# Stick-breaking attention by summation by parts, in a streaming encoder layer on one core

## The chip, the cores and the metric

The kernel runs on one core of a Trainium2 chip. Times are device microseconds from the core's run; lower is better. The engines are TensorE (PE; PEld is its weight load), VectorE (DVE), ScalarE (ACT), GpSimd (POOL) and SyncE (SP), which issues every DMA of this kernel.

## The reference

One layer of an encoder over 1,024 prompt frames and 64 frames of a running stream, 1,088 tokens in all, everything in float32. A mixer (three branches: stick-breaking attention, spatial gating, memory cross-attention) is followed by a feed-forward sublayer. The attention has 8 heads of 128 channels:

```python
def stick_breaking(q, k, v, q_pos, k_pos):
    # A[t,s] = beta_ts * prod_{s<j<t}(1-beta_tj), s < t only
    z = einsum('bqhd,bkhd->bhqk', q, k) * (SB_HEAD_DIM ** -0.5)
    mask = k_pos[None, :] < q_pos[:, None]
    log_keep = where(mask, log_sigmoid(-z), 0.0)
    between = cumsum(log_keep, axis=3, reverse=True) - log_keep
    w = where(mask, exp(log_sigmoid(z) + between), 0.0)
    return einsum('bhqk,bkhd->bqhd', w, v)
```

A prompt query sees the prompt keys before it. A sample query sees 256 cached keys and values and the sample's own before it. The new key and value rows are outputs too.

## The kernel before

Every instruction is emitted into a fixed order per engine by a program that runs while the kernel is built: it keeps a clock for each engine and one for the DMA bus (`Clocks`, with costs of its own), and places background work (`stream`, `breathe`, `later`) where those clocks say its inputs are ready. An engine then runs its instructions in that order and stops at the first whose inputs have not come. All instructions are recorded at line 75, the wrapper that accounts for them, so the rows are told apart by tile names.

**Projection.** The input projection is done in units of 256 output columns (`strassen_unit`): the seven products of a Strassen step, each of many matmuls into one of three PSUM buffers (`pb`), which DVE (and for the first product ACT) adds up into two row tiles `c[0]`, `c[1]` of 128 channels by 1,088 tokens. Weights arrive as two raw loads of 512 KB per unit, some products ahead, and ACT and DVE split them into a high and a low part (`whl`). The order of the projections is: gating values, gating input, memory queries, attention keys, attention values (four units, a pair of heads each), attention queries, gates.

**Values.** After a unit of attention values, `v_out` transposes each head's row tile to tokens on partitions (`transposed`: nine 128x128 blocks on PE, copied by ACT to a tile `tm` called `o` in the code). Then `fin` stores the output rows, stores the sample's 64 rows to `v8S`, and splits the 128x1,024 prompt part into a high and a low part (`vrh`, `vrl`), which go to DRAM (`vS`) and come back when the head is attended to.

**Attention.** `sb_all` runs 48 items, 8 heads by 6 batches of query blocks (128 queries each, as many keys as lie before them; the ninth block has 320 keys for the sample). In order of emission each step of the loop has: `z` of item n (scores on PE into PSUM, then ACT writes `pr` = sigmoid of the negated scores, which is the keep factor, and `beta` = sigmoid of the scores, and POOL zeroes the masked part of the diagonal blocks of `beta`), `trp` of item n-3 (PE transposes the weights; ACT copies the high part `ath`, DVE subtracts the low part `atl`), `scan` of item n-1 (DVE: a reverse running product of `pr`, which a mask resets to 1 at and beyond each query's position, then `beta` times the scanned product of the next key), and `av` of item n-4 (PE: weights times values; ACT writes `osb`). `sb_load` fetches the next head's keys, queries and values at its predecessor's first item, `sb_prep` prepares the cached keys at the third.

The last items run in the background of the branch projections that follow. Those are dense on TensorE, as is the feed-forward part.

Tiles come from rings of slots (`A`: 40 large slots, `U`: 11 small ones); a slot is used again when its last reader is done.

Of the kernel before, what the change touches and what calls it, by code (L numbers as in the profile page):

```python
# [9 lines left out]
F32 = mybir.dt.float32  # L10
F32R = mybir.dt.float32r
AF = mybir.ActivationFunctionType
ALU = mybir.AluOpType
AX = mybir.AxisListType

P = 128
T = 1088
# [67 lines left out]
class Clocks:  # L85
# [43 lines left out]
    def at(self, *tiles):  # L129
        return max([self.wrote.get(x.tensor.name, (0,))[0] for x in tiles], default=0) + self.LATENCY  # L130
# [16 lines left out]
def encoder_layer(  # L147
# [14 lines left out]
    clock, at = clocks.t, clocks.at  # L162
    nc = Engines(tc.nc, clocks)
    ctx.enter_context(tc.manual_schedule())

    keep = ctx.enter_context(tc.tile_pool(name="keep", bufs=1))
# [7 lines left out]
    def nm(s):  # L174
        cnt[0] += 1
        return f"{s}_{cnt[0]}"

    def A(shape, dt=F32, s="a"):
        return arena.tile(shape, dt, tag="s", name=nm(s), bufs=NSLOT)

    def U(shape, dt=F32, s="u"):
        return arena.tile(shape, dt, tag="u", name=nm(s), bufs=NSMALL)
# [17 lines left out]
    def dtile(shape, s):  # L200
        return dram.tile(shape, F32, tag=s, name=s)

    def f32(ap):
        return ap.bitcast(F32)
# [4 lines left out]
    def load(dst, src):  # L209
        nc.sync.dma_start(dst, src)  # L210

    def store(dst, src):
        nc.sync.dma_start(dst, src)

    def act(out, in_, f=AF.Copy, **kw):
        nc.scalar.activation(out, in_, f, **kw)

    def sub(out, a, b):
        nc.vector.tensor_tensor(out, a, b, op=ALU.subtract)
# [4 lines left out]
    def mul(out, a, b):  # L224
        nc.vector.tensor_tensor(out, a, b, op=ALU.mult)
# [19 lines left out]
    def tp(out, in_):  # L245
        n = in_.shape[0]
        nc.tensor.transpose(out, in_, ident[:n, :n])
# [7 lines left out]
    c_gmem, c_gpre, c_gffn, c_lng, c_lnb = [cols[:, 8 * i:8 * i + 8] for i in range(5)]  # L255
    c_gate = cols[:, 40:64]
    c_gpm, c_gpf = cols[:, 64:72], cols[:, 72:80]
    ones1 = keep.tile([P, 1], F32, tag="ones1", name="ones1")
    nc.vector.memset(ones1, 1.0)

# [6 lines left out]
    vS = [[dtile([P, 1024], f"vS{r}{p}") for p in "hl"] for r in range(8)]  # L267
    v8S = [dtile([64, P], f"v8S{r}") for r in range(8)]
# [14 lines left out]
    def later(n, fn, src=()):  # L283
        due.append((max([clock[e] for e in ("pe", "act", "dve")]) + 2.5 * n if n else at(*src), fn))
# [10 lines left out]
    def stream(*stages):  # L295
        st = list(stages)
        streams.append(st)
        return st
# [567 lines left out]
    def tm_store(dst_p, dst_s, h, o):  # L866
        store(dst_p[0, 0, :, h, :].rearrange("(j p) d -> p j d", p=P), o[:, :8, :])
        store(dst_s[0, 0, :, h, :], o[64:, 8, :])
# [12 lines left out]
    def v_out(p):  # L881
        def consume(c):
            for m in range(2):
                h = 2 * p + m

                def fin(o, h=h):
                    tm_store(sb_v_prompt, sb_v_sample, h, o)
                    store(v8S[h], o[64:, 8, :])
                    hi, lo = A([P, 1024], F32R, "vrh"), A([P, 1024], F32, "vrl")
                    ov = o[:, :8, :].rearrange("p j d -> p (j d)")  # L890
                    act(hi, ov)
                    sub(lo, ov, f32(hi))

                    later(0, lambda: store(vS[h][0], f32(hi)), [hi])
                    later(0, lambda: store(vS[h][1], lo), [lo])
                transposed(c[m], fin)
        return consume

# [827 lines left out]
    def sb_load(h):  # L1726
        s = SB[h] = {}
        for n, src, w in (("k", kT, T), ("q", qT, T), ("vv", vS, 1024)):
            pair = []
            for i in range(2):  # L1730
                t = A([P, w], F32, n)
                load(t, src[h][i])
                pair.append(f32r(t))
            s[n] = pair
            if n == "k":
                c = s["c"] = U([P, 4, P], F32, "sbc")
                load(c[:, :2], cache_sb_k[0, 0, :, h, :].rearrange("(m p) d -> p m d", p=P))
        load(c[:, 2:], cache_sb_v[0, 0, :, h, :].rearrange("(m p) d -> p m d", p=P))
        s["vv"] = [t.rearrange("p (j d) -> p j d", j=8) for t in s["vv"]]
        x = A([P, 768], F32, "ksv")  # L1740
        s["ks"] = f32r(x[:, :640]).rearrange("p (s m) -> p s m", s=2)
        s["v8"] = x[:, 640:]
        nc.gpsimd.memset(x[:64, 640:], 0.0)
        load(x[64:, 640:], v8S[h])

    def sb_prep(h):
        s = SB[h]
        t = PT()
        for m in range(2):
            tp(t[:, m * P:(m + 1) * P], s["c"][:, m, :])  # L1750
        ks = s["ks"]
        split(t[:, :256], ks[:, 0, :256], ks[:, 1, :256])
        for i in range(2):
            nc.gpsimd.tensor_copy(ks[:, i, 256:], f32(s["k"][i][:, 1024:]))
        s["prep"] = True


    BATCH = [[(0, 0), (2, 128), (1, 512)], [(3, 0), (8, 512)], [(4, 0)], [(5, 0)], [(6, 0)], [(7, 0)]]

    def length(i):  # L1760
        return 320 if i == 8 else (i + 1) * P
# [17 lines left out]
    def sb_all():  # L1779
        scale = 128 ** -0.5  # L1780
        masks = sb_masks()
        Ps, As, ATs, osb = {}, {}, {}, {}

        def z(h, b):
            s = SB[h]
            qh, ql = s["q"]
            pt = PB()
            base = 0
            L = sum(length(i) for i, _ in BATCH[b])
            for i, c in BATCH[b]:  # L1790
                kh, kl = s["k"] if i < 8 else (s["ks"][:, 0, :], s["ks"][:, 1, :])
                Li = length(i)
                qa = i * P if i < 8 else T - P

                parts = 1 if Li <= 512 else 2
                w = Li // parts
                wm = max(w, 256)
                if parts == 2:
                    base = 512 - w
                for q in range(parts):  # L1800
                    o = base + c + q * w
                    mm3(pt[:, o:o + wm], qh[:, qa:qa + P], ql[:, qa:qa + P], kh[:, q * w:q * w + wm],
                        kl[:, q * w:q * w + wm], True, True)
            beta = A([P, 1024], F32, "beta")
            pr = A([P, 1024], F32, "pr")
            zz = pt[:, base:base + L]
            act(pr[:, :L], zz, AF.Sigmoid, scale=-scale)
            act(beta[:, :L], zz, AF.Sigmoid, scale=scale)
            for i, c in BATCH[b]:
                dg = beta[:, c + length(i) - P:c + length(i)]  # L1810
                nc.gpsimd.affine_select(out=dg, in_=dg, pattern=[[-1, P]], base=0, channel_multiplier=1,
                                        compare_op=ALU.is_gt, fill=0.0)
            Ps[h, b], As[h, b] = pr, beta

        def scan(h, b):

            pr, beta = Ps.pop((h, b)), As[h, b]
            L = sum(length(i) for i, _ in BATCH[b])
            nc.vector.tensor_tensor_scan(pr[:, :L][:, ::-1], pr[:, :L][:, ::-1], masks[b][:, ::-1], 1.0,
                                         op0=ALU.mult, op1=ALU.max)  # L1820
            mul(beta[:, :L - 1], beta[:, :L - 1], pr[:, 1:L])

        def trp(h, b):
            a = As.pop((h, b))
# [35 lines left out]
        def av(h, g):  # L1860
            s = SB[h]
            pt = PT()
            if h not in osb:
                osb[h] = A([P, T], F32, "osb")
            if g == 8:
                f = ATs.pop((h, 8))
                for j in range(3):
                    vv = s["c"][:, 2 + j, :] if j < 2 else s["v8"]
                    nc.tensor.matmul(pt[:, :P], lhsT=vv, rhs=f[:, j, :], start=j == 0, stop=j == 2)
                act(osb[h][:, 1024:], pt[:, 64:P])  # L1870
                return
            vh, vl = s["vv"]
            at = ATs.pop((h, g))
            nb = 2 * g + 2
            for j in range(nb):
                hi, lo = at[j // 4]
                mm3(pt[:, :256], vh[:, j, :], vl[:, j, :], hi[:, j % 4, :], lo[:, j % 4, :], j == 0, j == nb - 1)
            act(osb[h][:, g * 256:(g + 1) * 256], pt[:, :256])
            if g == 3:
                o = osb.pop(h)  # L1880
                del SB[h]

                def put():
                    store(osc[0][h], o)
                    if h == 7:
                        O_READY[0] = 0
                later(0, put, [o])
# [6 lines left out]
        for n in range(N + SB_LAG + 1):  # L1894
            at_item[0] = n
            if n < N:
                h, b = items[n]
# [18 lines left out]
            if 0 <= n - SB_LAG - 1 < N:  # L1916
                h, b = items[n - SB_LAG - 1]
# [21 lines left out]
    for j in range(2):  # L1939
        d = {}  # L1940
# [12 lines left out]
    pt = PT()  # L1953
# [7 lines left out]
    for n, i in enumerate([0, 1, 2, 3, 8, 4, 5, 6, 7]):  # L1961
        def ld(i=i):
            H[i] = load_tile(i, x_prompt[0], x_sample[0])
        d = {}
# [105 lines left out]
```

## Time and profile before

| | us |
|---|---|
| median of 3 runs | 2312.54 |
| the runs | 2310.91 to 2314.28 |
| the profiled execution's own time | 2308.9 |
| its span, first to last instruction | 2306.3 |
| TensorE busy in the span | 2218.2 (96%) |
| VectorE busy in the span | 1600.3 (69%) |

The profile is of one execution. Shares of the whole span are averages over stages with different limits: the attention stage lies at about 960 to 1190 us, the projection of its values at about 450 to 560 us.

### The profile page before, as it was taken

How to read it: one execution, taken by the hardware profiler on the slowest of the kernel's cores; microseconds unless marked ns; L12 is line 12 of the kernel's file. 1: busy time of each engine (PE TensorE's matmuls, PEld its weight loads, DVE VectorE, ACT ScalarE, POOL GpSimd, SP SyncE). 2: the span in 40 equal slices, each digit the busy share in tenths (PEclk: the TensorE clock that was granted, in tenths of full speed). 3: DMA queues.
4: the chain of work that ended last, by engine and by line, in shares of the span. 5: the costliest groups of instructions: out<-in, count | busy, mean ns of one | idle time of the engine just before them, and what ended most of it. 6: DMA issues, size and time to landing. Idle time of an engine off the chain costs nothing. (4 is left out here: it accounts for less than half of the span.)

```text
span 2306.3 us, 40728 instructions
## 1 busy us (share of the span) xinstructions
PE 2218.2 (96%) x16465; PEld 2144.9 (93%) x16465; DVE 1600.3 (69%) x2483; ACT 781.4 (34%) x1383; POOL 143.8 (6%) x236
## 2 busy tenths in 40 slices
PE   7899999999999999988899999996999999999998
PEld 6799999999999999887799999996999999998886
DVE  7955688867776666699953443569777777774677
ACT  8442222333212223677731121344211111134353
POOL 2000000000000000134200000122000000000000
PEclk9999999999999999999999999998999999999999
DMA  6523356765393328654444352332323332247335
GB/s 206 183 89 101 123 207 208 230 202 199 144 298 133 113 86 287 254 205 165 143 159 128 112 170 86 104 108 92 94 83 104 94 102 87 92 159 275 83 106 187
DMA packets 249535, 345.97 MB, mean 150 GB/s; under 512 B 17140, under 2 KB 184644, under 8 KB 249348
## 3 DMA queue, kind: packets, MB, share of 16 engines
q1 hardware_dynamic: 249348, 343.38, 44.6%
q8 instruction: 130, 2.13, 0.4%
q14 instruction: 57, 0.47, 0.1%
HBM read 222.54 MB, written 120.78 MB: 149 GB/s over the span
## 5 line engine op out<-in xcount | busy, mean ns | idle before, releaser
L75 DVE TENSOR_TENSOR c<-pb,u 128x544 f32<-128x544 f32 (+2 forms) x236 | 168.4, 714 | 244.5 <-PE pb L75 232.2
L75 ACT ACTIVATE whl<-raw 128x512 fp32r<-128x512 f32 x254 | 157.1, 633 | 463.3 <-PE pb L75 185.5
L75 PE MATMUL pb<-fop,fop 128*128 128x512 f32 x924 | 219.3, 391 | 1.9 <-DVE p L75 1.6
L75 PEld LDWEIGHTS pb<-fop,fop 128*128 128x128 f32 x924 | 173.1, 188 | 40.4 <-DVE p L75 2.4
L75 DVE TENSOR_TENSOR whl<-raw,whl 128x512 fp32r<-128x512 f32 x286 | 193.3, 690 | 10.4 <-ACT whl L75 9.2
L75 DVE TENSOR_TENSOR u<-pb,u 128x544 f32<-128x544 f32 (+2 forms) x177 | 125.7, 710 | 66.3 <-PE pb L75 66.3
L75 DVE TENSOR_TENSOR whl<-u,whl 128x512 fp32r<-128x512 f32 x232 | 160.2, 690 | 6.0
L75 PE MATMUL pb<-XhB11a,whl 128*128 128x288 f32 x656 | 145.0, 297 | 0.6 <-ACT whl L75 0.4
L75 PE MATMUL pb<-XhB21a,whl 128*128 128x288 f32 x656 | 144.9, 297 | 0.0
L75 PE MATMUL pb<-XhB22a,whl 128*128 128x288 f32 x656 | 144.3, 295 | 0.0
L75 PE MATMUL pb<-XhB11b,whl 128*128 128x256 f32 x656 | 131.7, 284 | 0.0
L75 PE MATMUL pb<-XhB21b,whl 128*128 128x256 f32 x656 | 131.6, 284 | 0.0
L75 PE MATMUL pb<-XhB22b,whl 128*128 128x256 f32 x656 | 131.2, 283 | 0.0
L75 ACT ACTIVATE c<-c 128x1088 f32<-128x1088 f32 x38 | 42.4, 1115 | 226.8 <-DVE c L75 226.7
L75 PEld LDWEIGHTS pb<-XhB11a,whl 128*128 128x128 f32 x656 | 109.8, 188 | 1.1 <-ACT whl L75 0.6
L75 PEld LDWEIGHTS pb<-XhB22a,whl 128*128 128x128 f32 x656 | 109.9, 188 | 0.0
L75 PEld LDWEIGHTS pb<-XhB21a,whl 128*128 128x128 f32 x656 | 109.8, 188 | 0.0
L75 PE MATMUL pb<-Xrh,whl 128*128 128x288 f32 (+1 forms) x512 | 102.6, 296 | 6.9 <-DVE whl L75 6.9
L75 PEld LDWEIGHTS pb<-XhB21b,whl 128*128 128x128 f32 x656 | 107.7, 191 | 0.0
L75 PEld LDWEIGHTS pb<-XhB22b,whl 128*128 128x128 f32 x656 | 107.6, 191 | 0.0
L75 PEld LDWEIGHTS pb<-XhB11b,whl 128*128 128x128 f32 x656 | 107.3, 190 | 0.1
L75 PE MATMUL pb<-XhT1a,whl 128*128 128x288 f32 x464 | 102.2, 296 | 0.6 <-DVE sgo L75 0.6
(327 smaller groups left out, 6378.4 us busy)
## 6 DMA issues: line engine op xcount, KB each, us to landing
raw<-in_w_in_dram SPq DMA_DIRECT2D x72, 512.0 KB
raw<-in_w_ffn_in_dram SPq DMA_DIRECT2D x88, 256.0 KB
gsc<-c SPq DMA_DIRECT2D x24, 544.0 KB
grow<-gsc SPq DMA_DIRECT2D x24, 544.0 KB
raw<-in_w_branch_dram SPq DMA_DIRECT2D x24, 512.0 KB
fS<-fsum SPq DMA_DIRECT2D x44, 256.0 KB
fw<-in_w_ffn_out_dram SPq DMA_DIRECT2D x44, 256.0 KB
fa<-fS SPq DMA_DIRECT2D x44, 256.0 KB
```

The lines of the kernel that those rows point to most:

```text
L75: r = fn(*a, **k)
```

## The change

With S_s the product of the keep factors from key s up to the query, the weight of key s is S_(s+1) - S_s. Summed by parts, the output is the sum over s of S_s (v_(s-1) - v_s), with v before the first key taken as zero, plus the last value before the query. The scan already yields S_s, and yields 1 where the key is not before the query; there the differences telescope, so that adding the value of the last row of each 128-query block (`vlast`, one column per block and head) completes the sum.

So `z` no longer computes `beta` nor selects on it, and `scan` no longer multiplies; `trp` transposes the scanned `pr` itself. `av` writes `osb` with `vlast` as a bias, one 128-column block at a time. `v_out` now writes 16 small columns on ACT, and `fin` builds the shifted values `w` in a new tile (`tmv`): a one-row memset, then copies by DMA of `o` moved down by one row: rows 0 to 126 of all eight prompt blocks to rows 1 to 127, row 127 of each block to row 0 of the next, 63 rows of the sample's block, and one row of the value cache. A stage on DVE then subtracts `o` from `w`, splits the result and has it stored. `sb_load` also loads the cached values moved by one row (a tile `sbb`; its first copy has 127 rows too), and `sb_prep` subtracts.

```diff
@@ -255,6 +255,8 @@
     c_gmem, c_gpre, c_gffn, c_lng, c_lnb = [cols[:, 8 * i:8 * i + 8] for i in range(5)]
     c_gate = cols[:, 40:64]
     c_gpm, c_gpf = cols[:, 64:72], cols[:, 72:80]
+
+    vlast = keep.tile([P, 8, 9], F32, tag="vlast", name="vlast")
     ones1 = keep.tile([P, 1], F32, tag="ones1", name="ones1")
     nc.vector.memset(ones1, 1.0)
 
@@ -883,16 +885,30 @@
             for m in range(2):
                 h = 2 * p + m
 
+                act(vlast[:, h, :8], c[m][:, :1024].rearrange("p (j q) -> p j q", j=8)[:, :, P - 1])
+                act(vlast[:, h, 8:], c[m][:, T - 1:])
+
                 def fin(o, h=h):
                     tm_store(sb_v_prompt, sb_v_sample, h, o)
-                    store(v8S[h], o[64:, 8, :])
-                    hi, lo = A([P, 1024], F32R, "vrh"), A([P, 1024], F32, "vrl")
-                    ov = o[:, :8, :].rearrange("p j d -> p (j d)")
-                    act(hi, ov)
-                    sub(lo, ov, f32(hi))
-
-                    later(0, lambda: store(vS[h][0], f32(hi)), [hi])
-                    later(0, lambda: store(vS[h][1], lo), [lo])
+
+                    w = A([P, 9, P], F32, "tmv")
+                    nc.gpsimd.memset(w[:1, 0, :], 0.0)
+                    load(w[1:, :8, :], o[:P - 1, :8, :])
+                    load(w[:1, 1:8, :], o[P - 1:, :7, :])
+                    load(w[65:, 8, :], o[64:P - 1, 8, :])
+                    load(w[64:65, 8, :], cache_sb_v[0, 0, 255:, h, :])
+
+                    def steps_():
+                        sub(w[:, :8, :], w[:, :8, :], o[:, :8, :])
+                        sub(w[64:, 8, :], w[64:, 8, :], o[64:, 8, :])
+                        later(0, lambda: store(v8S[h], w[64:, 8, :]), [w])
+                        hi = A([P, 8, P], F32R, "vrh")
+                        ov = w[:, :8, :]
+                        act(hi, ov)
+                        sub(o[:, :8, :], ov, f32(hi))
+                        later(0, lambda: store(vS[h][0], f32(hi).rearrange("p j d -> p (j d)")), [hi])
+                        later(0, lambda: store(vS[h][1], o[:, :8, :].rearrange("p j d -> p (j d)")), [o])
+                    stream(("dve", lambda: at(w), steps_))
                 transposed(c[m], fin)
         return consume
 
@@ -1736,6 +1752,10 @@
                 c = s["c"] = U([P, 4, P], F32, "sbc")
                 load(c[:, :2], cache_sb_k[0, 0, :, h, :].rearrange("(m p) d -> p m d", p=P))
         load(c[:, 2:], cache_sb_v[0, 0, :, h, :].rearrange("(m p) d -> p m d", p=P))
+        b = s["cb"] = U([P, 2, P], F32, "sbb")
+        nc.gpsimd.memset(b[:1, 0, :], 0.0)
+        load(b[1:, 0, :], cache_sb_v[0, 0, :P - 1, h, :])
+        load(b[:, 1, :], cache_sb_v[0, 0, P - 1:2 * P - 1, h, :])
         s["vv"] = [t.rearrange("p (j d) -> p j d", j=8) for t in s["vv"]]
         x = A([P, 768], F32, "ksv")
         s["ks"] = f32r(x[:, :640]).rearrange("p (s m) -> p s m", s=2)
@@ -1748,6 +1768,7 @@
         t = PT()
         for m in range(2):
             tp(t[:, m * P:(m + 1) * P], s["c"][:, m, :])
+        sub(s["c"][:, 2:], s.pop("cb"), s["c"][:, 2:])
         ks = s["ks"]
         split(t[:, :256], ks[:, 0, :256], ks[:, 1, :256])
         for i in range(2):
@@ -1779,7 +1800,7 @@
     def sb_all():
         scale = 128 ** -0.5
         masks = sb_masks()
-        Ps, As, ATs, osb = {}, {}, {}, {}
+        As, ATs, osb = {}, {}, {}
 
         def z(h, b):
             s = SB[h]
@@ -1801,24 +1822,17 @@
                     o = base + c + q * w
                     mm3(pt[:, o:o + wm], qh[:, qa:qa + P], ql[:, qa:qa + P], kh[:, q * w:q * w + wm],
                         kl[:, q * w:q * w + wm], True, True)
-            beta = A([P, 1024], F32, "beta")
-            pr = A([P, 1024], F32, "pr")
-            zz = pt[:, base:base + L]
-            act(pr[:, :L], zz, AF.Sigmoid, scale=-scale)
-            act(beta[:, :L], zz, AF.Sigmoid, scale=scale)
-            for i, c in BATCH[b]:
-                dg = beta[:, c + length(i) - P:c + length(i)]
-                nc.gpsimd.affine_select(out=dg, in_=dg, pattern=[[-1, P]], base=0, channel_multiplier=1,
-                                        compare_op=ALU.is_gt, fill=0.0)
-            Ps[h, b], As[h, b] = pr, beta
+            pr = As[h, b] = A([P, 1024], F32, "pr")
+            act(pr[:, :L], pt[:, base:base + L], AF.Sigmoid, scale=-scale)
 
         def scan(h, b):
 
-            pr, beta = Ps.pop((h, b)), As[h, b]
+
+
+            pr = As[h, b]
             L = sum(length(i) for i, _ in BATCH[b])
             nc.vector.tensor_tensor_scan(pr[:, :L][:, ::-1], pr[:, :L][:, ::-1], masks[b][:, ::-1], 1.0,
                                          op0=ALU.mult, op1=ALU.max)
-            mul(beta[:, :L - 1], beta[:, :L - 1], pr[:, 1:L])
 
         def trp(h, b):
             a = As.pop((h, b))
@@ -1867,7 +1881,7 @@
                 for j in range(3):
                     vv = s["c"][:, 2 + j, :] if j < 2 else s["v8"]
                     nc.tensor.matmul(pt[:, :P], lhsT=vv, rhs=f[:, j, :], start=j == 0, stop=j == 2)
-                act(osb[h][:, 1024:], pt[:, 64:P])
+                act(osb[h][:, 1024:], pt[:, 64:P], AF.Identity, bias=vlast[:, h, 8:])
                 return
             vh, vl = s["vv"]
             at = ATs.pop((h, g))
@@ -1875,7 +1889,9 @@
             for j in range(nb):
                 hi, lo = at[j // 4]
                 mm3(pt[:, :256], vh[:, j, :], vl[:, j, :], hi[:, j % 4, :], lo[:, j % 4, :], j == 0, j == nb - 1)
-            act(osb[h][:, g * 256:(g + 1) * 256], pt[:, :256])
+            for i in range(2 * g, 2 * g + 2):
+                act(osb[h][:, i * P:(i + 1) * P], pt[:, (i % 2) * P:(i % 2 + 1) * P], AF.Identity,
+                    bias=vlast[:, h, i:i + 1])
             if g == 3:
                 o = osb.pop(h)
                 del SB[h]
```

## Rows read from the trace of the kernel before

**Rows 1.** The page: busy share of each engine, then TensorE in 40 slices, in tenths.

```profile
PE 2218.2 (96%) x16465; PEld 2144.9 (93%) x16465; DVE 1600.3 (69%) x2483; ACT 781.4 (34%) x1383; POOL 143.8 (6%) x236
...
PE   7899999999999999988899999996999999999998
```

**Rows 2.** Busy time by stretch: attention, then its DVE-bound middle, then its end.

```profile
960.00:1190.00 230.00, 199.04 (x1430) 184.66 (x1429) 210.57 (x244) 153.01 (x286) 73.35 (x159) 0.99 0.50 180
...
1000.00:1150.00 150.00, 124.45 (x894) 114.62 (x895) 146.23 (x158) 105.12 (x192) 54.31 (x120) 0.98 0.46 165
...
1140.00:1150.00 10.00, 4.61 (x21) 4.22 (x21) 9.81 (x11) 5.74 (x8) 1.05 (x2) 0.68 0.44 128
```

**Rows 3.** VectorE's instructions by group, 960 to 1190 us.

```profile
L75 DVE TENSOR_TENSOR_SCAN pr<-pr,mask 128x640 f32<-128x640 f32 (+3 forms) x32 | 60.3, 1883 | 0.0
...
L75 DVE TENSOR_TENSOR beta<-beta,pr 128x767 f32<-128x767 f32 (+4 forms) x48 | 50.8, 1059 | 5.2 <-POOL beta L75 0.5
...
L75 DVE TENSOR_TENSOR atl<-pb,ath 128x512 fp32r<-128x512 f32 (+2 forms) x96 | 48.6, 547 | 6.2 <-ACT ath L75 6.0 <-PE pb L75 0.3
...
L75 DVE TENSOR_TENSOR ksv<-pt,ksv 128x256 fp32r<-128x256 f32 x8 | 3.3, 418 | 1.7 <-ACT ksv L75 1.7
```

**Rows 4.** TensorE's transposes and longest waits, 960 to 1190 us.

```profile
L75 PE MATMUL pb<-ident,beta 128*128 128x128 f32 x312 | 43.4, 278 | 28.0 <-DVE beta L75 27.4
...
POOL beta L75 <- ACT beta L75: 114.1, 41, 7.9
...
PE pb L75 <- DVE beta L75: 27.4, 22, 4.2
```

**Rows 5.** ScalarE and GpSimd groups that the change touches, 960 to 1190 us.

```profile
L75 ACT ACTIVATE beta<-pb 128x768 f32<-128x768 f32 (+4 forms) x48 | 41.4, 863 | 0.0
...
L75 ACT ACTIVATE osb<-pt 128x256 f32<-128x256 f32 (+1 forms) x39 | 14.2, 368 | 25.6 <-PE pt L75 25.3
...
L75 POOL TENSOR_SCALAR_AFFINE_SELECT beta<-beta 128x128 f32<-128x128 f32 x72 | 53.4, 757 | 120.0 <-ACT beta L75 114.1 <-issue 5.9
```

**Rows 6.** Busy time while values are projected, then ten microseconds of heavy transfers.

```profile
460.00:560.00 100.00, 100.00 (x802) 99.35 (x801) 68.67 (x101) 33.67 (x56) 1.68 (x5) 1.00 0.62 206
...
890.00:900.00 10.00, 10.00 (x82) 10.00 (x81) 5.96 (x10) 1.75 (x3) 0.00 (x0) 1.00 1.04 401
```

**Rows 7.** SP's DMA issues in order of time, one pair of value heads.

```profile
476.74 0.60 SPq L75 DMA_DIRECT2D v8S<-tm  x1
...
481.71 1.35 SPq L75 DMA_DIRECT2D v8S<-tm  x1
...
484.48 2.12 SPq L75 DMA_DIRECT2D raw<-in_w_in_dram  x2
```

**Rows 8.** VectorE in order of time in the same unit.

```profile
481.44 1.22 DVE L75 TENSOR_TENSOR vrl<-tm,vrh 128x1024 f32<-128x1024 f32 x1
...
482.58 0.72 DVE L75 TENSOR_TENSOR c<-pb,u 128x544 f32<-128x544 f32 x1
...
487.55 0.72 DVE L75 TENSOR_TENSOR u<-pb,u 128x544 f32<-128x544 f32 x1 [0.51 <-PE pb L75]
```

**Rows 9.** TensorE in order of time: first matmuls of five products.

```profile
473.94 0.38 PE L75 MATMUL pb<-XhB11a,whl 128*128 128x288 f32 x1
...
478.19 0.38 PE L75 MATMUL pb<-XhB21a,whl 128*128 128x288 f32 x1
...
487.35 0.30 PE L75 MATMUL pb<-XhT1a,whl 128*128 128x288 f32 x1
...
493.40 0.30 PE L75 MATMUL pb<-XhT4a,whl 128*128 128x288 f32 x1
...
497.23 0.38 PE L75 MATMUL pb<-XhB11a,whl 128*128 128x288 f32 x1
```

**Rows 10.** DMA issues of one tile: cached values for the sample's queries.

```profile
L75 SPq DMA_DIRECT2D sbc<-in_cache_sb_v_dram x8: 424/446/732, 956.7 to 1104.3; - x8
```

## The prediction

> **What bounds the kernel now.** The page comes first. TensorE is busy in 96% of the span [rows 1], so what a stage can give back is mostly what TensorE stands idle in it. The digits are nines but for a few slices, and the eights at the 16th to 18th are the attention stage.
>
> The busy time by stretch [rows 2] says who makes TensorE wait there. From 1000 to 1150 us VectorE works 146.2 of 150 us, TensorE 124.5, ScalarE 105.1: attention is VectorE's stage, with TensorE second. From 960 to 1190 us TensorE is idle 230.0 - 199.0 = 31.0 us.
>
> VectorE's groups [rows 3] are the scan (60.3 us in the 32 large items, more in the 16 packed ones), the product with `beta` (50.8 us) and the subtraction of low parts (48.6 us). TensorE's transposes stand idle 28.0 us in all, 27.4 of it for VectorE's `beta`, and GpSimd waits 114.1 us for ScalarE, which costs nothing by itself [rows 4]. So nearly all of the 31.0 us is the transpose waiting for a weight that VectorE has not multiplied.
>
> The projection of the values is the other place that the change touches. There TensorE is busy 100.00 of 100 us and VectorE 68.7 [rows 6]: whatever stops TensorE in this stage is lost in full.
>
> **Attention, part by part.** The product goes: 48 x 1.059 us = 50.8 us of VectorE [rows 3]. `sb_prep` gains a subtraction of 128x256; the nearest row, the 128x256 one of `ksv`, takes 0.418 us, so 8 x 0.418 = 3.3 us. VectorE's 210.6 us [rows 2] become about 163, TensorE keeps 199.0, and TensorE becomes the bound. The second sigmoid goes too, 41.4 us of ScalarE [rows 5]. Splitting the 32 evictions of 128x256 in two adds to ScalarE at least nothing and at most another 0.37 us each, 12 us; ScalarE then has some 124 of 230 us, so neither counts. The selection (53.4 us of GpSimd) is off the path: GpSimd itself is the one that waits [rows 4, 5].
>
> The gain is at most the 31.0 us. The transposes still wait for a scan of 1.9 us that stands behind a subtraction in VectorE's order, with VectorE loaded to four fifths, and in the last ten microseconds before 1150 the splits for the next branch fill VectorE (9.81 of 10 us, TensorE 4.61 at a granted clock of 0.68 [rows 2]). I keep 25 us; the lower end is 15, if half of the waits come back as waits for the scan. The shifted cache copy (`sbb`, one copy of 127 rows of 512 bytes) is issued once a head, and a head is (1104.3 - 956.7)/7 = 21.1 us [rows 10]; even at the slow price below it is 65,024 bytes / 25 GB/s = 2.6 us, and it is needed at the third of the head's six items, some 7 us later. Nothing.
>
> **Values: the arithmetic.** Each head gains one 128x1024 subtraction, 1.22 us by the row of `vrl` [rows 8], and a 64-row one of 128 elements, below 0.42 us: 8 x 1.64 = 13 us into the 31 us that VectorE is idle in 100 us [rows 6]. ScalarE's 16 small copies go into 66 us of idle time. Hidden, as long as VectorE isn't held up.
>
> **Values: the copies.** What can hold it up is the new tile `w`. VectorE runs in a fixed order, and the build's clocks place the subtraction about 5 us after the copies are issued. Behind it in that order stand the evictions of PSUM and the splits of weights, and TensorE waits for those. So the price is how late `w` lands.
>
> The large copy moves 127 rows of 4,096 bytes, 520,192 bytes. In the busiest stretch the sixteen DMA engines move 401 GB/s at a share of 1.04 [rows 6], 25 GB/s each. If the copy is spread over all sixteen it takes 1.3 us; if one engine carries all of it, 20.8 us. No copy of the kernel before shows which: their row counts (128, 64, 32, 24, 8) can be cut into equal shares for several engines, and 127 is a prime and cannot. Between ends this far apart I take the one-engine end, because equal shares are the one arrangement that every copy here allows.
>
> The Trainium skill states the rule (DMA: Bandwidth & Descriptors, section "Why a DMA increments its semaphore by 16 and not by 1"): a copy runs on the largest number of engines, up to 16, that divides the outermost count on both sides, and "127 partitions" gives 1. It speaks against this change: without it the sum below would end near 2288 us, with it near 2412. No row here shows it.
>
> Now one unit with its pair of heads. TensorE's unit starts at 473.94 and the next at 497.23 [rows 9], 23.3 us for seven products, 3.3 each. The first head's `o` is stored by 476.74 + 0.60 = 477.3 us and the second's by 481.71 + 1.35 = 483.1 [rows 7]; there the copies go out. Ahead of each in the engine's queue is its share of the output rows, 524,288 bytes / 401 GB/s = 1.3 us.
>
> First copy: 477.3 + 1.3 + 20.8 = 499.4. Its subtraction stands in VectorE's order at about 482, ahead of the eviction at 482.58 [rows 8]. With three PSUM buffers TensorE can go on until it wants the buffer of that eviction, at the product that began at 487.35 [rows 9]. VectorE is free again at 499.4 + 1.5 (subtractions) and evicts (0.72) by 501.6. TensorE is 501.6 - 487.35 = 14.3 us late.
>
> Second copy: it follows the first on the same engine, 499.4 + 1.3 + 20.8 = 521.5. Its subtraction stands at about 487, ahead of the eviction at 487.55 [rows 8], and holds the product that began at 493.40 [rows 9]. That one now begins at 521.5 + 1.5 + 0.7 = 523.7, which is 30.3 us late, the 14.3 included. The next unit's raw weights, issued at 484.48 [rows 7], come behind it in the same queue, at 521.5 + 2 x 1.3 = 524 us, and are split by about 526, before their first product (497.23 + 30.3 = 527.5): no more is lost for them, but nothing is caught up either.
>
> The next pair is stored only when TensorE has transposed it, so the delay repeats: four pairs x 30.3 = 121 us.
>
> TensorE's clock adds to that. In the ten microseconds after which it had stood 4 us idle the granted clock is 0.68, a loss of 3.2 us [rows 2]. Here each pair has two pauses; the loss after the first is covered by the second copy, so four of 2 to 3 us: 10.
>
> **The sum.** 2308.9 (the profiled execution's own time) - 25 + 121 + 10 = 2414.9. The median of the runs is 3.6 us above that execution. Against it stands the bandwidth of one engine alone, which may lie above its share of a contended 401 GB/s; each GB/s more takes 0.8 us off a copy, some 6 us off the whole. I predict 2412 us.
>
> By the skill's page one engine moves about 27 GiB/s, an estimate of 18 us for the copy; the sum by that would be some 23 us lower.
>
> **Rivals.**
>
> *The copies are spread, or hidden.* If they land within about 5 us as the build's clocks assume, the stage stays dense and only the gain is left: 2312.5 - 25 = 2288 us. It decides below about 8 us per copy (5 us of planned distance and some 5 of PSUM cover, less 1.5 of subtractions), that is, with three engines or more. For it: VectorE's 31% of idle time and the DMA share of 0.62 [rows 6]. Against it: the prime count. Chance 0.10. This is the side on which the change is faster.
>
> *One engine, but half of it covered.* If the subtractions fall later in VectorE's order, or the second copy's wait overlaps the catching up, a pair costs about 15 us: 4 x 15 = 60, and 2312.5 - 25 + 60 = 2348 us. For it: the position of the subtractions is read from clocks that I don't run. Against it: the second copy alone lands 38 us after its `o`, more than a unit. Chance 0.08.
>
> *The copies hold up the weights as well.* The stores of the split values now wait for VectorE in SP's order; if the raw loads come behind them, they go out only after the second landing and a pair costs 38 to 42 us: 2312.5 - 25 + 160 + 10 = 2458 us. For it: SP issues the raw loads right behind the first head's stores now [rows 7]. Chance 0.07.
>
> *Attention gains nothing* (another wait, say for PSUM, takes the product's place): 2412 + 25 = 2437 us. For it: all of TensorE's idle time sits on one pair of tiles, so what is next is unseen. It lies in the range and I give it no chance of its own.
>
> **How the numbers follow.** The forecast has 0.75, the three rivals 0.10, 0.08 and 0.07. The range 2365 to 2455 holds the forecast with its bounds (attention 15 to 31, a copy 10% either way of 20.8 us, the cover of a pair 4 to 8 us off) and the nearer parts of the second and third rival, about 0.8 in all. A change of 0.2%, 4.6 us, is about what a measurement of this kernel can tell from none. Faster: 0.10; the same would need half-covered copies that just eat the gain: 0.02; slower: 0.88.
>
> **What the profile after would show.** Right: between 477 and 550 us of old time VectorE's longest waits are for the DMA into `tmv`, twice a pair and some 15 us each; TensorE's digits drop there, the granted clock dips, and the time from issue to the first subtraction is above 20 us while the mean DMA share is low. The projection of the values and the unit after it last about 120 us longer. Attention is some 25 us shorter, VectorE below 90% in its middle and TensorE above 95%. Wrong: no wait for `tmv` above 3 us would mean the copies are spread, and the time 2288; a wait of TensorE for raw weights as long as that for VectorE would mean the third rival; transposes that still wait 20 us for `pr` would mean that the attention step fell short.

## The result and the profile after

The changed kernel takes 2426.28 us (median of 4 runs, 2425.57 to 2429.71), the kernel before 2311.72 us on the same chip (4 runs, 2309.88 to 2314.28). The ratio is 1.0498, 95% interval 1.0479 to 1.0516: 114.6 us slower. The median lies 14.3 us above the forecast 2412 and inside 2365 to 2455. The profiled execution took 2425.8 us.

Three marks split the span: the first VectorE instruction that writes `sgo` (its stage follows the values), the first sigmoid `pr` on ScalarE (attention begins) and the last write of `osb` (attention ends). In us from the span's start:

| | before | after | difference |
|---|---|---|---|
| first `sgo` | 647.1 | 789.0 | +141.9 up to here |
| first `pr` | 967.9 | 1109.5 | -0.3 between |
| last `osb` | 1192.4 | 1308.1 | -25.9 in attention |
| end of the span | 2306.3 | 2424.1 | +2.1 behind it |

So the loss lies in the values and the gain in attention, as forecast. The page of the kernel after, with the rows that answer to [rows 1], and the granted clock:

```profile
PE 2239.7 (92%) x16465; PEld 2166.5 (89%) x16465; DVE 1565.2 (65%) x2459; ACT 756.9 (31%) x1383; POOL 97.0 (4%) x180
...
PE   7899999954459999999999999998899999999998
...
PEclk9999999977679999999999999999999999999999
```

TensorE's digits fall in the ninth to twelfth slice, the values, together with its clock. The eights of attention are gone. By stretch (answers to [rows 2, 6]; attention stands 141.6 us later than before):

```profile
480.00:500.00 20.00, 7.53 (x61) 7.32 (x59) 0.72 (x1) 0.00 (x0) 0.00 (x0) 0.75 0.17 54
500.00:520.00 20.00, 9.44 (x48) 8.89 (x48) 6.33 (x9) 1.57 (x2) 0.00 (x0) 0.67 0.29 102
520.00:540.00 20.00, 14.20 (x94) 13.70 (x95) 11.46 (x18) 6.73 (x15) 0.39 (x2) 0.73 0.35 119
...
1160.00:1240.00 80.00, 80.00 (x607) 76.75 (x606) 71.34 (x83) 54.38 (x120) 13.86 (x50) 1.00 0.59 215
```

From 480 to 500 us VectorE works 0.72 us and ScalarE nothing, while the sixteen DMA engines are busy to 0.17 and move 54 GB/s. All compute waits for transfers, and the transfers leave most of the DMA engines idle. In attention TensorE is busy 80.00 of 80 us and VectorE 71.34: the bound has moved as the prediction said.

SP's issues in the same unit (answer to [rows 7]; start, us from the first to the end of the last of a run, queue, what):

```profile
475.57 1.13 SPq L75 DMA_DIRECT2D out_dram<-tm  x2
476.81 10.32 SPq L75 DMA_DIRECT2D tmv<-tm  x3
...
487.72 9.56 SPq L75 DMA_DIRECT2D out_dram<-tm  x2
497.73 11.06 SPq L75 DMA_DIRECT2D tmv<-tm  x3
...
511.38 1.11 SPq L75 DMA_DIRECT2D raw<-in_w_in_dram  x1
...
522.12 0.38 SPq L75 DMA_DIRECT2D raw<-in_w_in_dram  x1
...
533.83 1.14 SPq L75 DMA_DIRECT2D out_dram<-tm  x2
```

The same pair of stores of `tm` comes for the fourth pair at 650.06, so a pair takes (650.06 - 475.57)/3 = 58.2 us, 34.9 more than the 23.3 of before. VectorE, ScalarE and TensorE in that pair (answers to [rows 8, 9]; in brackets the idle time before and what ended it):

```profile
481.59 0.72 DVE L75 TENSOR_TENSOR c<-pb,u 128x544 f32<-128x544 f32 x1 [3.19 <-PE pb L75]
500.42 1.54 DVE L75 TENSOR_TENSOR tmv<-tmv,tm 128x1024 f32<-128x1024 f32 x2 [18.11 <-DMA tmv<-tm]
...
522.37 1.55 DVE L75 TENSOR_TENSOR tmv<-tmv,tm 128x1024 f32<-128x1024 f32 x2 [14.67 <-DMA tmv<-tm]
```

```profile
501.73 1.06 ACT L75 ACTIVATE vrh<-tmv 128x1024 fp32r<-128x1024 f32 x1 [22.41 <-DVE tmv L75]
502.69 0.61 ACT L75 ACTIVATE whl<-u 128x512 fp32r<-128x512 f32 x1
...
524.64 1.13 ACT L75 ACTIVATE whl<-raw 128x512 fp32r<-128x512 f32 x2
527.63 0.63 ACT L75 ACTIVATE whl<-raw 128x512 fp32r<-128x512 f32 x1 [1.86 <-DMA raw<-in_w_in_dram]
```

```profile
503.35 0.61 PE L75 MATMUL pb<-XhT1a,whl 128*128 128x288 f32 x1 [15.82 <-ACT whl L75]
...
525.31 0.61 PE L75 MATMUL pb<-XhT4a,whl 128*128 128x288 f32 x1 [12.02 <-ACT whl L75]
```

The two subtractions start at 500.42 and 522.37, for forecast landings at 499.4 and 521.5. But TensorE does not wait for a PSUM buffer, as forecast. The eviction of 481.59 ran ahead of the subtraction. TensorE waits for a split weight, `whl`, and that stands in *ScalarE's* order behind `vrh`, which waits 22.41 us for the subtraction. The two products that began at 487.35 and 493.40 [rows 9] begin at 503.35 and 525.31: 16.0 and 31.9 us late (forecast 14.3 and 30.3). Over all pairs, 460 to 690 us (who waited for whom: us in total, times, longest):

```profile
ACT vrh L75 <- DVE tmv L75: 151.1, 7, 22.8
DVE tmv L75 <- DMA tmv<-tm: 116.7, 7, 18.5
...
PE pb L75 <- ACT whl L75: 99.9, 7, 16.2
...
ACT whl L75 <- DMA raw<-in_w_in_dram: 11.6, 4, 6.0
```

The weights' own loads cost ScalarE only 11.6 us, 6.0 of it ahead of the first copy. So the third rival's price did not come, although the raw loads went out at 511.38 and 522.12 and not at 484.48 [rows 7]. Attention by group, 1109 to 1309 us (answers to [rows 3 to 5]), and the issues of the shifted cache copy (beside [rows 10]; min/median/max in ns):

```profile
L75 DVE TENSOR_TENSOR atl<-pb,ath 128x512 fp32r<-128x512 f32 (+2 forms) x96 | 48.8, 551 | 27.4 <-ACT ath L75 25.0 <-PE pt L75 2.3
...
L75 DVE TENSOR_TENSOR sbc<-sbb,sbc 128x256 f32<-128x256 f32 x8 | 3.3, 410 | 8.2 <-DMA sbb<-in_cache_sb_v_dram 8.2
...
L75 PE MATMUL pb<-ident,pr 128*128 128x128 f32 x312 | 42.3, 274 | 2.0 <-DVE pr L75 2.0
...
L75 ACT ACTIVATE osb<-pt,vlast 128x128 f32<-128x128 f32 (+1 forms) x72 | 22.7, 364 | 36.8 <-PE pt L75 36.5
...
L75 SPq DMA_DIRECT2D sbb<-in_cache_sb_v_dram x16: 250/2700/6266, 1099.0 to 1228.9; - x16
```

TensorE's transposes stand idle 2.0 us instead of 28.0, and it is VectorE that now waits (27.4 us), which costs nothing while TensorE is full. Half an `osb` costs 364 ns, where a whole one cost 368 [rows 5]: 22.7 us against 14.2, within the bound of 12 us more.

### The profile page after: what moved, and what is told of

The parts are those of the page before. It is cut to its first block, busy times and chain, and to the rows that moved or that the text cites. A ratio compares the mean times of both kernels' runs of the same rounds, so it can differ in the third digit from the quotient of the medians.

```text
span 2424.1 us, 40682 instructions
## 1 busy us (share of the span) xinstructions
PE 2239.7 (92%) x16465; PEld 2166.5 (89%) x16465; DVE 1565.2 (65%) x2459; ACT 756.9 (31%) x1383; POOL 97.0 (4%) x180
## 5 line engine op out<-in xcount | busy, mean ns | idle before, releaser
L75 PE MATMUL pb<-XhT1a,whl 128*128 128x288 f32 x464 | 108.1, 308 | 67.0 <-ACT whl L75 63.8
L75 PE MATMUL pb<-XhT4a,whl 128*128 128x288 f32 x464 | 108.0, 308 | 51.1 <-ACT whl L75 49.1
L75 PEld LDWEIGHTS pb<-XhT1a,whl 128*128 128x128 f32 x464 | 81.3, 197 | 69.3 <-ACT whl L75 65.9
L75 PEld LDWEIGHTS pb<-XhT4a,whl 128*128 128x128 f32 x464 | 81.3, 197 | 53.4 <-ACT whl L75 49.9
```

Of the source, the lines that this page charges most:

```text
L75: r = fn(*a, **k)
```

## The experiments

Two theories stood against each other. *The order*: the copy is slow, and the loss is that engines stand at their first instruction that needs it. *The queue*: the copy holds up what is issued behind it, so the loss comes even if nobody waits for the copy itself. Behind both stands the claim that a 127-row copy runs on one DMA engine. All experiments but one start from the kernel after; the long copy is `load(w[1:, :8, :], o[:P - 1, :8, :])`.

| run | what | us | ratio to before, 95% |
|---|---|---|---|
| e1_even | both 127-row copies as 112 + 15 rows | 2284.80 | 0.9881 (0.9865 to 0.9898) |
| e2_four | long copy as 124 + 3 | 2315.12 | one run |
| e3_two | long copy as 122 + 5 | 2343.06 | one run |
| e7_unread | before, with the long copy unread | 2460.78 | one run |
| e4_cache | long copy cut, cache copy not | 2283.90 | 0.9882 (0.9864 to 0.9900) |
| e5_sigmoid | e1 with the second sigmoid | 2290.20 | 0.9909 (0.9894 to 0.9923) |
| e6_product | e1 with a product after each scan | 2312.56 | one run |
| e9_pool | long copy uncut, issued by GpSimd | 2288.91 | one run |
| e10_late | long copy uncut, subtractions planned later | 2426.63 | one run |
| e11_spread | e1, next branch's loads spread | 2289.80 | 0.9912 (0.9895 to 0.9928) |

One run has no interval. Single executions of the kernel before, taken beside these, lie between 2308.2 and 2314.8 us.

### Row counts: e1_even, e2_four, e3_two

```diff
-                    load(w[1:, :8, :], o[:P - 1, :8, :])
+                    load(w[1:113, :8, :], o[:112, :8, :])
+                    load(w[113:, :8, :], o[112:P - 1, :8, :])
```

and the first `sbb` copy likewise. In e2 the cut is at 124 and in e3 at 122 rows, with `sbb` as in e1.

> The changed kernel with each copy of 127 rows cut in two, 112 rows and 15, for the shifted values and for the shifted cache. If the loss comes from copies that only one DMA engine carries, the waits of VectorE for the shifted values fall below 3 us each, the projection of the values is as dense as before, and the time is 2288 us (2283 to 2294), faster than both kernels. If the loss comes from waiting for any copy between tiles at this place (landing time, VectorE's order), the time stays above 2380 us. If attention's gain was only a shift of work out of a stage that was stalled anyway, the time is 2312 us.

> The shifted values are copied as 124 rows and 3; the shifted cache is even. If equal shares decide, 124 rows run on four engines and take 5.1 us: that is inside the planned distance of 5 us and the cover of TensorE, so the time is 2290 us (2286 to 2300). If the number of rows doesn't matter and only the cut does, it is the time of the even kernel as well; if 112 rows are fast for another reason (a multiple of 16 needed), it is above 2400 us.

> The shifted values are copied as 122 rows and 5; the shifted cache is even. Equal shares: 122 rows on two engines, 10.2 us a copy; the two of a pair hold TensorE up for some 11 us, 2288 + 4 x 11 + 10 for the clock = 2342 us (2315 to 2360), between the even kernel and the changed one. If a copy is either spread or not, without steps between, the time is 2290 or 2420 us.

e1 gave 2284.80 us, faster than both kernels. VectorE and SP in the first pair, and the two stretches of e1 that answer to [rows 6] and to attention's middle:

```profile
483.98 1.54 DVE L75 TENSOR_TENSOR tmv<-tmv,tm 128x1024 f32<-128x1024 f32 x2
```

```profile
478.56 3.63 SPq L75 DMA_DIRECT2D tmv<-tm  x4
...
484.17 3.36 SPq L75 DMA_DIRECT2D tmv<-tm  x4
```

```profile
460.00:560.00 100.00, 99.08 (x789) 97.70 (x788) 74.42 (x110) 34.87 (x72) 2.80 (x13) 1.00 0.71 226
...
1000.00:1100.00 100.00, 100.00 (x754) 95.73 (x753) 89.17 (x104) 68.87 (x152) 15.70 (x61) 1.00 0.61 218
```

The subtraction starts at 483.98 without a wait (no bracket), SP issues four copies in 3.6 us where three took 10.3, and the clock stays at 1.00. The same bytes cut otherwise are worth 141.5 us. The marks of e1 are 651.9, 972.6, 1168.4 and 2279.4: the values cost 4.8 us more than before, attention gives 28.7.

By the Trainium skill (DMA: Bandwidth & Descriptors, section "Why a DMA increments its semaphore by 16 and not by 1") a copy uses the largest number of engines, at most 16, that divides the outermost count of both sides; for 127, 122, 124 and 112 rows that is 1, 2, 4 and 16. The runs agree with it: 2426, 2343, 2315 and 2285 us.

e3 fell on its expectation (2342), e2 missed it by 25. Their waits for the copy, 460 to 690 us, e2 and then e3:

```profile
ACT vrh L75 <- DVE tmv L75: 42.2, 6, 9.6
...
DVE tmv L75 <- DMA tmv<-tm: 22.3, 5, 6.4
```

```profile
ACT vrh L75 <- DVE tmv L75: 69.3, 7, 12.5
...
DVE tmv L75 <- DMA tmv<-tm: 46.0, 7, 8.6
```

At 124 rows the copy is still late five times. Over e1 a pair of heads costs (2315.12 - 2284.80)/4 = 7.6 us in e2, 14.6 in e3 and 35.4 uncut: the cost falls with the row count's divisor, but the cover on which the forecast let it vanish ("three engines or more") isn't there. In e2 the first subtraction of a pair waits 5.1 us and TensorE 2.9. From 476 us to the first `sgo` TensorE is idle 17.0 us in e2 and 1.1 in e1, and it is busy 185.0 us at a granted clock of 0.94 against 174.9 at 1.00. So of the 26.2 us that the values cost more in e2, some 16 are stops and some 10 the lower clock.

### Is a waiting reader needed: e7_unread, e10_late

```diff
                     store(v8S[h], o[64:, 8, :])
+                    w = A([P, 9, P], F32, "tmv")
+                    load(w[1:, :8, :], o[:P - 1, :8, :])
```

This is the kernel before plus one long copy per head into a tile that nothing reads.

> The kernel before with the 127-row copy of each value head into a tile that nothing reads; no instruction of VectorE or ScalarE waits for it. If the loss comes through VectorE's fixed order (the subtraction that stands ahead of evictions and splits), this costs at most 10 us: 2312 to 2322 us. If the one engine's queue is enough by itself, because the next unit's weights come behind both copies in it, the weights land some 27 us late for each pair and the time is 2410 us (2390 to 2430).

In e10 the long copy is uncut (the cache copy is cut as in e1) and the build places the subtractions 18 us later:

```diff
-                    stream(("dve", lambda: at(w), steps_))
+                    stream(("dve", lambda: at(w) + 18, steps_))
```

> The changed kernel with its uncut copies of the shifted values (the shifted cache is even), but the subtractions of both heads of a pair planned 18 us later, which puts them behind the next unit's first product, some 20 us further back in VectorE's and ScalarE's order. If the loss comes through the order of VectorE and ScalarE, a pair loses at most 10 us: 2285 + 4 x 10 + 5 = 2330 us (2300 to 2345). If the one engine's queue and SP behind it are enough, as the unread copies suggest, the time is still 2410 to 2440 us.

Eight unread copies cost 149 us, more than the whole change and more than either expectation. So the order with its subtractions isn't needed for the loss. e7 doesn't separate the causes cleanly, though, because the copies also keep slots taken: nothing else holds the slot of the unread tile, and the copy is one more reader of `tm`, so the next writer of such a slot waits for the copy (the rows don't tell which of the two slots it is). Waits of e7, 460 to 690 us, then its SP issues:

```profile
DVE whl L75 <- DMA raw<-in_w_in_dram: 64.0, 3, 21.8
...
DVE c L75 <- DMA tmv<-tm: 35.1, 2, 17.8
```

```profile
478.77 0.71 SPq L75 DMA_DIRECT2D tmv<-tm  x1
479.84 8.35 SPq L75 DMA_DIRECT2D vS0h<-vrh  x1
...
489.89 11.20 SPq L75 DMA_DIRECT2D out_dram<-tm  x2
...
512.02 8.75 SPq L75 DMA_DIRECT2D raw<-in_w_in_dram  x2
```

35.1 us are for a slot, 64.0 for raw weights that SP issues at 512.02 instead of 484.48 [rows 7]. In each of the first three pairs TensorE stops 13.4 to 13.9 us behind the first wait and 17.8 to 18.6 us behind the second. e10 takes the reader out of the way in its first pair. There the first unit goes on past the place of the subtractions, and this is what stops it (SP, then ScalarE, VectorE and TensorE, each in order of time):

```profile
478.70 10.30 SPq L75 DMA_DIRECT2D tmv<-tm  x3
...
489.61 9.49 SPq L75 DMA_DIRECT2D out_dram<-tm  x2
499.54 11.09 SPq L75 DMA_DIRECT2D tmv<-tm  x3
...
512.01 5.23 SPq L75 DMA_DIRECT2D raw<-in_w_in_dram  x2
```

```profile
526.17 0.63 ACT L75 ACTIVATE whl<-raw 128x512 fp32r<-128x512 f32 x1 [39.10 <-DMA raw<-in_w_in_dram]
```

```profile
526.84 0.69 DVE L75 TENSOR_TENSOR whl<-raw,whl 128x512 fp32r<-128x512 f32 x1 [32.99 <-ACT whl L75]
```

```profile
528.22 1.11 PE L75 MATMUL pt<-ident,c 128*128 128x128 f32 x4 [29.27 <-DVE c L75]
```

The chain reads backwards: TensorE waits 29.27 us for VectorE, that for ScalarE, that for raw weights, issued at 512.01 behind the copies. No subtraction of shifted values stands in it. In the kernel after, the readers' order stops TensorE 15.82 + 12.02 us in the same pair. Two waits thus lie side by side: take the reader out of the way and the weights behind the copies take its place. In this pair the queue alone is enough; in the kernel after the readers' order ends last.

The later pairs of e10 show less, for another wait comes in (ScalarE, then TensorE, third pair):

```profile
610.50 0.63 ACT L75 ACTIVATE whl<-u 128x512 fp32r<-128x512 f32 x1 [31.93 <-DMA vS2h<-vrh]
611.18 0.61 PE L75 MATMUL pb<-XhT1a,whl 128*128 128x288 f32 x1 [25.34 <-ACT whl L75]
```

This split doesn't read `vrh`, but it waits for the store of it, so it waits for a slot. The store comes late behind the late subtractions, which are e10's own edit, and behind the copies in SP's order. From 460 to 700 us TensorE stops some 70 us behind such slots (15.94, 25.34, 17.64 and 11.22 us). That the time, 2426.63, is that of the kernel after to 0.4 us is therefore a coincidence. What the queue alone would cost over all four pairs, with no slot in the way, neither run shows.

### The other 127-row copy: e4_cache

Here the long copy is cut as in e1, the cache copy stays whole.

> The changed kernel with the shifted values cut into 112 rows and 15, but the shifted cache still loaded with one copy of 127 rows of 512 bytes a head. At 2.6 us on one engine, issued some 7 us before it is wanted, it costs nothing: 2285 us, the time of the even kernel (2282 to 2288). If its 127 pieces hold up SP as the large copies do, eight heads lose 3 to 6 us each: 2310 to 2330 us.

2283.90 us against 2284.80: no difference that can be measured. Its waits for `sbb` are 7.0 us (3 times) against 3.6 (2 times) in e1. The small copy costs nothing, as forecast.

### What bounded attention: e5_sigmoid, e6_product

```diff
             act(pr[:, :L], pt[:, base:base + L], AF.Sigmoid, scale=-scale)
+            act(A([P, 1024], F32, "beta")[:, :L], pt[:, base:base + L], AF.Sigmoid, scale=scale)
```

(e5; its result is not read.) In e6, behind the scan, a product of the old size whose result is not read either:

```diff
+            mul(A([P, 1024], F32, "beta")[:, :L - 1], pr[:, 1:L], pr[:, 1:L])
```

> The even kernel with the second sigmoid put back, written to a tile that nothing reads. If attention gained by VectorE's product alone, ScalarE's 41 us are hidden and the time is 2285 us (2282 to 2289). If the second sigmoid was on the path (it stands ahead of the copy of the high parts on ScalarE), attention is 10 us longer or more: above 2295 us.

> The even kernel with a product of the old size put back after each scan, on VectorE, from the scanned tile into one that nothing reads; no engine waits for its result. If VectorE's load was the bound, the 51 us come back as in the kernel before and the time is 2285 + 25 = 2310 us (2304 to 2316). If what counted was the transpose's wait for the product's result, the time stays at 2285 to 2290 us.

From 1000 to 1100 us, e5 and then e6 (PE, PEld, DVE, ACT, POOL; then clock, DMA share, GB/s):

```profile
1000.00:1100.00 100.00, 98.68 (x715) 91.28 (x712) 83.93 (x99) 82.75 (x171) 15.93 (x60) 1.00 0.59 214
```

```profile
1000.00:1100.00 100.00, 89.07 (x625) 80.21 (x624) 99.10 (x113) 57.23 (x124) 13.55 (x49) 1.00 0.49 175
```

With the product back VectorE is full (99.10 of 100), TensorE falls to 89.07, and from the first `pr` to the last `osb` it takes 1190.7 - 972.1 = 218.6 us, 22.8 more than e1's 195.8. The transposes stand idle only 3.8 us in e6, since the added product's result isn't waited for: it is VectorE's load that counts. The second sigmoid makes the whole 5 us longer, 4.7 of it in attention (1170.6 - 970.1 = 200.5 us), between the two expectations (2285 and above 2295); TensorE loses 1.3 of 100 us with ScalarE at 82.75. That the loss is ScalarE's evictions coming later is argued, not shown.

### Another issuer: e9_pool

```diff
-                    load(w[1:, :8, :], o[:P - 1, :8, :])
+                    nc.gpsimd.dma_start(w[1:, :8, :], o[:P - 1, :8, :])
```

(`sbb` cut as in e1.)

> The changed kernel with the 127-row copy of the shifted values issued by GpSimd and not by SP, uncut; the shifted cache is even. If GpSimd's copies are shared out over all engines whatever the count, the time is that of the even kernel, 2285 us, or up to 10 us more for a longer issue. If they are shared by equal parts as SP's are, one engine carries each copy, SP itself is not held by the issue of it but the weights still queue behind it on that engine, and the time is 2380 to 2430 us.

2288.91 us: uncut, but issued by GpSimd, the copy costs hardly more than cut. VectorE waits 0.5 us for it from 460 to 690 us. The queue's line on the page of e9 (packets, MB, share of 16 engines):

```profile
q0 software_dynamic: 1152, 4.16, 0.7%
```

The 4.16 MB are the eight copies of 520,192 bytes. The first is issued at 476.57 and its subtraction runs at 483.54, 7.0 us later, where SP's copy needed over 20. That is at least 74 GB/s, three times the 25 GB/s of one engine's share: GpSimd's copy is spread over several engines.

The Trainium skill names this exception in the same section (DMA: Bandwidth & Descriptors, "Why a DMA increments its semaphore by 16 and not by 1"): copies issued through GpSimd may be dealt to sixteen engines in groups of rows, 127 partitions among them. The run agrees as far as it goes; how many engines the copy had, it doesn't show.

### Beyond e1: e11_spread

In e1 attention's last stretch still stalls: from 1110 to 1130 us TensorE is busy 15.75 of 20 us at a clock of 0.83. Here the next branch's loads and splits begin at item 38, two items apart, instead of at 43:

```diff
-                if b == 1 and h == 7:
+                if n == 38:
...
-                        for st in load_o(BR[0], t, s, lambda i=i: at_item[0] >= O_FIRST + i * O_GAP):
+                        for st in load_o(BR[0], t, s, lambda i=i: at_item[0] >= 38 + 2 * i):
```

> The even kernel with the loads and splits of the next branch's input begun five items earlier and two items apart, so that their 12 us of VectorE are spread over the last ten items of attention and not over the last four. TensorE's idle time and half clock around 1110 to 1130 us (about 4 us idle and 3 us of clock in the even kernel) should go, if VectorE, now 90% loaded, can take the splits in between: 2279 us (2276 to 2284). If VectorE is as full there, TensorE waits elsewhere for as long and the time is 2285 us.

It missed: 2289.80 us, 5 slower than e1. In the same 20 us TensorE is busy 10.50. Its longest stop there is 4.57 us for ScalarE's `ath`; why that came late was not followed up.

## Why the prediction was right, point by point

**The size of a copy: right.** Forecast landings 499.4 and 521.5, subtractions at 500.42 and 522.37. The two readers start 22.0 us apart, some 24 GB/s for 520,192 bytes: one engine's share of a contended 401 GB/s was the right price, and no allowance for more bandwidth was needed. That the row count is the cause is shown by e1, e2 and e3.

**The place of the wait: wrong.** The step was "Its subtraction stands in VectorE's order at about 482, ahead of the eviction at 482.58" and the PSUM buffer from it. The eviction came first. What stopped TensorE was a weight split on ScalarE behind `vrh`, an order that the forecast never looked at. It read VectorE's timeline for what stands behind the new wait, but the step that waits puts an instruction on ScalarE too. The delay came out alike because both chains begin at the same landing and, by luck, stop the same two products.

**"No more is lost for them": true and misleading.** Behind the copies of the kernel after, raw weights cost ScalarE 5.6 us in three waits. But the step had them issued at 484.48, and they went out at 511.38 and 522.12, since SP was held behind the copies, which the forecast did not have. They hide under the readers' wait, and in e10's first pair they alone stop TensorE for 29.3 us. The rival that priced them at 38 to 42 us a pair had them issued only after the second landing; the last one went out about then (522.12, the subtraction at 522.37), and the two waits overlap.

**A pair: 34.9 us instead of 30.3.** Of the 4.6 us by which this term was mis-sized, 0.9 is the second landing and 0.7 the path from it to TensorE (31.9 late instead of 30.3): it takes 525.31 - 522.37 = 2.9 us through ScalarE, for 2.2 forecast. The other 3.0 lie behind that product, where the granted clock is 0.73 and ScalarE still waits 1.86 us for raw weights; the forecast had 2.5 for the clock, in a term of its own. That term was read from ten microseconds in which TensorE worked only 4.61 us [rows 2], so its 3.2 us was no measured loss, and that 2.5 came near is luck. Over the whole stage, from 476 us to the first `sgo`, TensorE is idle 116.8 us and busy 196.2, in e1 idle 1.1 and busy 174.9: of the 137.1 us between the two some 116 are stops and some 21 the lower clock, part of it under the second copies, as forecast. Values and clock together: 131 forecast, 141.9 measured. As e1 shows, 4.8 us of that remain without the slow copy.

**Attention: right.** -25.9 us for -25, with TensorE as the new bound; e1 gives 28.7, near the full 31.0. The bound was worked out; the 25 was judged, between 15 and 31, so that it came this near is in part luck. e6 puts 22.8 of it down to VectorE's product, e5 some 5 to the sigmoid, which the forecast had at nothing. (The eights of [rows 1] that the prediction gives to attention stand at the 18th to 20th slice, not at the 16th to 18th; nothing rests on that.)

**The rival of spread copies: its time right, its condition wrong.** e1 and e9 give 2285 and 2289 for 2288. But at four engines 30 us are still lost, so "three engines or more" was too easy. The cover was taken as planned distance plus a PSUM buffer, and no PSUM buffer was what ended the wait.

**The sum.** 2308.9 + 141.9 - 25.9 + 2.1 - 0.3 = 2426.7 (the profiled execution: 2425.8; the marks are of the span, and the time outside it is 0.9 us shorter after). Of the 14.3 us by which the median lies above 2412, 10.9 are the values with the clock, and 2.9 are the two allowances at the end, 3.6 up for the median and some 6 down for bandwidth: the median is 0.5 us above the profiled execution, and no more bandwidth came.

## What to carry to other kernels

Before a shifted copy goes into a stage that is full on TensorE, look at its row count: here 127 rows cost 35 us a pair, and 112 + 15 rows of the same bytes next to nothing. A late transfer is priced at every engine's order that its readers stand in and at the queue behind it, and those prices overlap, so removing one wait may show the next at full length. Where a loss hides a gain, as 142 us hid 26 here, take the loss out by itself: e1 and e4, 1.2% faster than before, are this change with a copy or two cut in two.

## What the hardware showed unexpectedly

SP itself is held: with one-engine copies outstanding, a group of three issues takes 10.0 to 11.9 us (eight groups of the kernel after), two plain stores behind it 8.8 to 9.7 in the first three pairs, where four issues of cut copies take 3.4 to 4.4 in e1 and 4.8 to 6.0 in e2. In e7 the issue right behind the copy takes 8.35 us, though it moves other data. So the copies are late to be issued as well as slow, and everything behind them in SP's order too. What holds an issue was not separated out.

TensorE's granted clock fell to 0.67 in 500 to 520 us, after 20 us in which it worked 7.53, that is, part of the time at the lower of its two levels (1.2 and 2.4 GHz); from 476 to 700 us it averages 0.71. In e1 it is 1.00 over the values. Between the two it is worth some 21 us.
